# A two-layer transformer on one core: weights split in whole buffers of 2048 columns instead of halves

## The chip, the cores and the metric

The kernel runs on one core of one Trainium2 chip. The metric is device time in microseconds. The engines are TensorE (PE in the profile; its weight loads are PEld), VectorE (DVE), ScalarE (ACT), GpSimd (POOL) and SyncE (SP, which issues most of the loads).

## The reference

Input is one sequence of 256 tokens of width 1024 in float32. Two layers run one after the other, each of three blocks that add to the residual `x`:

```python
for l in range(2):
    x = x + 0.5 * swiglu(rms_norm(x, ffa_norm[l]), ffa_w_gate[l], ffa_w_up[l], ffa_w_down[l])
    x = x + hybrid_mixer(rms_norm(x, mix_norm[l]), w_in[l], ..., w_out[l])
    x = x + 0.5 * swiglu(rms_norm(x, ffb_norm[l]), ffb_w_gate[l], ffb_w_up[l], ffb_w_down[l])
return rms_norm(x, final_norm)
```

`swiglu` is `(silu(x @ w_gate) * (x @ w_up)) @ w_down` with an inner width of 2816. `hybrid_mixer` projects to 2840 columns (`w_in`), runs two kinds of attention on 8 heads each, and projects back with `w_out`. All weights are float32, and each is used once, so each comes once from memory.

## The kernel before

**Split products.** Every float32 product is made of three matmuls of a rounded type (`F32R`). A factor w is split into `whi`, its rounded copy, and `wlo`, the rest `w - whi`; `prod3` (lines 321 to 326) adds x-high times w-high (line 323), x-high times w-low (line 324) and x-low times w-high (line 325) into one PSUM bank. `prod_t` (lines 334 to 343, matmuls at 340 to 342) is the same with the weight as the stationary side. So weights have to be split on the way: ACT copies raw columns into `whi` (line 304), DVE subtracts (line 283). `xhi`/`xlo`, `hhi`/`hlo`, `nhi`/`nlo`, `ohi`/`olo` and `fnhi`, `fohi` are split left sides.

**Units.** Weights come in units of at most 2048 columns on 128 partitions, 1 MB each. A unit is loaded by one transfer, mostly, into one of five `raw` buffers (`loader`), or is added by a transfer onto the raw buffer that holds an earlier unit (`adder`, line 263, issued by POOL). `Unit` holds the state of one: `part(i)` gives the slices of high and low for row block i, `when(i)` the event after which they may be read. Before, a unit's high and low lie in two pairs of tiles of 1024 columns (`halves`). There are NW = 6 such tiles for `whi` and six for `wlo`; one token of the pool `"w"` stands for a pair, and `free_w` gives one back. Most units are split 1024 columns at a time (`step` = 2 quarters). The units of Q, D and E in the mixer (`grouped`) and the first two of the program (`fine`) are split a quarter at a time, 512 columns.

**Who orders the work.** The program's order on every engine is written out by a planner (`Flow`) that runs when the kernel is built: coroutines yield events or buffer tokens, each engine has a modelled clock, and among those that are due the one with the lowest rank goes first. It decides only the order in which instructions are put into each engine's queue; on the chip each engine takes its own queue in order and waits for the semaphores of its operands. `splitter` (lines 268 to 306, rank 4) walks the units in order: it waits until ACT and DVE are nearly free, writes the DVE subtraction of the piece before (`low`), waits for the landed raw columns and a token, and writes the ACT copy of the next piece. The main coroutine walks the products in a fixed order and waits for `when(i)`.

**The stages.** In an FFN, gate and up columns run in the order of `PLANS`: names such as `g2` or `u2` are two units each whose quarters meet both token halves, 24 matmuls of 512 columns for a unit; names such as `51` are one unit with one token block, 12 matmuls. The down projection follows `DOWN`: `1d` to `7d` are units of 12 matmuls, `p2` to `p10` units of 24. At the end of an FFN (`TAIL`) the units `p7` and `p10` are walked once for each of four output banks and stay held to the end, and `4d` is used ahead of the fourth of these walks. In the mixer, the projections `A Q B D E F`, the attention, and the output projection `out_prod` follow; that holds both units of a half (first n, then m) until all of its four banks are done. After each block, `close` or `out_close` adds to `x`, `Norm.pair` turns `x` (line 409), makes `xhi` and `xlo` (lines 415, 418) and squares (line 431) for the next block.

Of the kernel before, what the change touches and what calls it, by code (L numbers as in the profile page):

```python
# [9 lines left out]
F32R = mybir.dt.float32r  # L10
I32 = mybir.dt.int32
BF16 = mybir.dt.bfloat16
AF = mybir.ActivationFunctionType
# [121 lines left out]
def hybrid_kernel(ctx, tc, x_in, ffa_norm, ffa_w_gate, ffa_w_up, ffa_w_down, mix_norm, w_in,  # L135
# [3 lines left out]
    nc = tc.nc  # L139
# [3 lines left out]
    wts = ctx.enter_context(tc.tile_pool(name="wts", bufs=4))  # L143
# [4 lines left out]
    ctx.enter_context(tc.manual_schedule())  # L148

    fl = Flow()  # L150
    NRAW, NW, NP = 5, 6, 5
    for tag, n in (("acc", 4), ("sb", 2), ("tb", 2), ("raw", NRAW), ("w", NW),
                   ("work", 7), ("p", NP), ("pT", 4), ("pair", 1)):
        fl.pool(tag, range(n))
# [22 lines left out]
    class Raw:  # L177


        def __init__(self, src, a, b, loads=1):  # L180
            self.src, self.a, self.b, self.loads = src, a, b, loads
            self.landed = [Event() for _ in range(4)]
            raws.append(self)
# [15 lines left out]
    class Unit:  # L199
# [3 lines left out]
        def __init__(self, raw, done=True, fine=False, grouped=False):  # L203
            self.raw, self.a, self.b = raw, raw.a, raw.b
            self.done, self.grouped = done, grouped
            self.step = 1 if fine or grouped else 2
            self.ready, self.halves = [Event() for _ in range(4)], []
            self.over = Event()
            units_.append(self)

        def part(self, i):

            k = self.a // 2
            return [z[:, i % k * self.b:(i % k + 1) * self.b] for z in self.halves[i // k]]

        def when(self, i):
            return self.ready[4 * (i + 1) // self.a - 1]
# [50 lines left out]
    def splitter():  # L268

        def view(u, z, i, turned=False):  # L270
            m = u.a * u.b // 4
            z = z[:, i % 2 * m:(i % 2 + u.step) * m]
            if not u.grouped:
                return z
            return z.rearrange("p (r g d) -> p g r d" if turned else "p (g r d) -> p g r d", r=4, g=2)

        def source(u, i):
            src = u.raw.rows(i, u.step)
            return src.rearrange("p (g r d) -> p g r d", g=2, r=4) if u.grouped else src

        def low(u, i, t):
            hi, lo = u.halves[i // 2]
            nc.vector.tensor_tensor(view(u, lo, i, True), source(u, i), view(u, hi.bitcast(F32), i, True), OP.subtract)  # L283
            e = fl.dve(u.step * u.a * u.b // 4, after=t)
            for j in range(i, i + u.step):
                u.ready[j].set(e)
            if i + u.step == 4:
                u.over.set(e)
                if u.done:
                    fl.put("raw", 0, e)  # L290

        last = None
        for u in units_:
            for i in range(0, 4, u.step):
                yield max(fl.eng["act"], fl.eng["dve"]) - (TH if fl.clock > 16.0 else TH0)
                if last is not None:
                    low(*last)
                    last = None
                yield u.raw.landed[i + u.step - 1]
                if i % 2 == 0:  # L300
                    yield fl.get("w")
                    u.halves.append(tuple(wts.tile([128, 1024], F32R, name=z, tag=z, bufs=NW) for z in ("whi", "wlo")))
                n = u.step * u.a * u.b // 4
                nc.scalar.activation(view(u, u.halves[-1][0], i, True), source(u, i), AF.Copy)  # L304
                last = (u, i, fl.act(n))
        low(*last)

    def copy(dst, src, n):
# [3 lines left out]
        nc.vector.tensor_copy(dst, src)  # L312
        return fl.dve(n)

    def free_w(u=None):
        fl.put("w", 0)

    def cols(w, c0, n, kh):
        return w[kh * 512:(kh + 1) * 512, c0:c0 + n].rearrange("(k p) n -> p k n", p=128)
# [171 lines left out]
    def ffn(us, nm, nxt, plan, last=False):  # L491
# [103 lines left out]
        def plain(z, tag, first):  # L595
            c, then = int(z[1:]), {"g": gate, "u": up, "h": both}[z[0]]
            ps = {}
            for kh in range(2):
                u = us[z, kh]
                order_ = [(t, i) for t in range(T) for i in range(4)] if first and nm.gi else [(t, i) for i in range(4) for t in range(T)]  # L600
                for t, i in order_:
                    k = kh * 4 + i
                    yield nm.turned[k, t]
                    yield u.when(i)
                    if k == 0:
                        yield fl.get(tag)
                        ps[t] = bank(tag, 4 if tag == "acc" else 2)
                    prod(ps[t], nm.xs, t, k, u, i, slice(0, 512), k == 0, k == KT - 1)
                    if k == KT - 1:
                        fl.spawn(then(c, t, ps[t], tag))  # L610
                    yield
                    if t and i % 2:
                        free_w()
# [55 lines left out]
        def product(p, c):  # L669
            u = us[p, c]  # L670
            key = dict(zip("1265374", "aabccdd"))[p]
            if p == "1":
                fl.spawn(rest(c))
                fl.spawn(gate0(c))
            start = p in "1657"
            k0, t = {"1": (0, 0), "2": (4, 0), "4": (4, 1)}.get(p, (0, 0))
            if p in "124":
                left = [z[:, k0:k0 + 4, t * 128:(t + 1) * 128] for z in nm.xs]
                for k in range(k0, k0 + 4):
                    yield nm.turned[k, t]  # L680
            else:
                yield event("form", p)
                left = forms[p]
            if not start:
                yield event(key, c)
            for i in range(4):
                yield u.when(i)
                if i == 0 and start:
                    yield fl.get("acc")
                    bk[key, c] = bank("acc", 4)  # L690
                wh, wl = u.part(i)
                prod3(bk[key, c], left[0][:, i], left[1][:, i], wh, wl, start and i == 0, i == 3)
                yield
                if i % 2:
                    free_w()
            event("P" + p, c).set(fl.clock + HOP)
# [67 lines left out]
        def down(j, t, cs, free):  # L764
            u = us["d", j]
            yield ev[j // 2, t]
            for c in cs:
                new = yield from bank_d(t, c)
                for i in range(2):
                    k = 2 * j + i  # L770
                    yield u.when(i)
                    prod(pd[t, c], hs, t, k, u, i, slice(c * 512, (c + 1) * 512), new and i == 0, k == 21)
                    yield
            if free:
                free_w()
                free_w()
# [961 lines left out]
    for q in range(4):  # L1738
        fl.spawn(start_x(q))
    fl.spawn(loader(), 3)  # L1740
    fl.spawn(splitter(), 4)
    fl.spawn(adder(), 3)
    fl.spawn(main(), 5)
# [38 lines left out]
```

## Time and profile before

| what | us |
|---|---|
| median of 2 runs | 993.69 (993.49 to 993.89) |
| the profiled execution | 991.77 |
| its span, first to last instruction | 990.0 |
| busy: PE, DVE, ACT, POOL | 980.0, 799.9, 643.4, 68.9 |
| weights and inputs read | 215.09 MB |

Busy time counts an engine from the start of an instruction to its end. Matmuls overlap in the pipeline and their ends are modelled, so for PE the distance from start to start is to be read, not only the busy share. In a timeline row the note in brackets is the idle time of the engine ahead of that row and what ended it.

### The profile page before, as it was taken

How to read it: one execution, taken by the hardware profiler on the slowest of the kernel's cores; microseconds unless marked ns; L12 is line 12 of the kernel's file. 1: busy time of each engine (PE TensorE's matmuls, PEld its weight loads, DVE VectorE, ACT ScalarE, POOL GpSimd, SP SyncE). 2: the span in 40 equal slices, each digit the busy share in tenths (PEclk: the TensorE clock that was granted, in tenths of full speed). 3: DMA queues.
4: the chain of work that ended last, by engine and by line, in shares of the span. 5: the costliest groups of instructions: out<-in, count | busy, mean ns of one | idle time of the engine just before them, and what ended most of it. 6: DMA issues, size and time to landing. Idle time of an engine off the chain costs nothing.

```text
span 990.0 us, 14315 instructions
## 1 busy us (share of the span) xinstructions
PE 980.0 (99%) x5236; PEld 820.0 (83%) x5236; DVE 799.9 (81%) x1458; ACT 643.4 (65%) x1101; POOL 68.9 (7%) x73
## 2 busy tenths in 40 slices
PE   9999999999999999999999999999999999999997
PEld 8888888898987888888888888888988878888885
DVE  6977786797887978798798778877878789688976
ACT  7665555568785676666567566646787766665654
POOL 1010001100000011101001110101000001110110
PEclk9999999999999999999999999999999999999999
DMA  9889679463743699989859999893645337999891
GB/s 336 267 211 282 221 196 288 127 217 115 265 138 116 188 252 287 259 255 244 258 174 238 293 272 253 228 302 110 225 170 200 101 128 216 278 272 278 252 213 43
DMA packets 109831, 217.08 MB, mean 219 GB/s; under 512 B 3928, under 2 KB 23520, under 8 KB 109760
## 3 DMA queue, kind: packets, MB, share of 16 engines
q1 hardware_dynamic: 85584, 168.50, 48.6%
q0 software_dynamic: 23872, 47.12, 27.0%
q8 instruction: 41, 0.67, 0.3%
q10 hardware_dynamic: 304, 0.53, 0.1%
q14 instruction: 30, 0.25, 0.1%
HBM read 215.09 MB, written 1.05 MB: 218 GB/s over the span
## 4 chain that ended last, share of the span: by engine, by line
PE 98%; DVE 1%; ACT 1%; issue 0%; POOL 0%; POOLq 0%
PE acc L323 18%; PE acc L324 18%; PE acc L325 18%; PE sb L325 8%; PE sb L323 8%; PE sb L324 8%; PE acc L340 2%; PE acc L341 2%; PE acc L342 2%; PE tb L555 2%; PE acc L1209 2%; PE tb L1189 2%; PE tb L409 1%; PE acc L1378 1%; PE sb L1315 1%; PE sb L1258 1%
## 5 line engine op out<-in xcount | busy, mean ns | idle before, releaser
L283 DVE TENSOR_TENSOR wlo<-raw,whi 128x1024 fp32r<-128x1024 f32 (+2 forms) x422 | 472.2, 1139 | 116.3 <-ACT whi L304 115.7
L304 ACT ACTIVATE whi<-raw 128x1024 fp32r<-128x1024 f32 (+2 forms) x422 | 408.6, 993 | 200.6 <-PE acc L325 75.3
L323 PE MATMUL acc<-whi,xhi 128*128 128x512 f32 (+1 forms) x372 | 145.8, 392 | 0.0
L324 PE MATMUL acc<-wlo,xhi 128*128 128x512 f32 (+1 forms) x372 | 142.0, 382 | 0.0
L325 PE MATMUL acc<-whi,xlo 128*128 128x512 f32 (+1 forms) x372 | 141.9, 381 | 0.0
L323 PE MATMUL sb<-whi,xhi 128*128 128x512 f32 x288 | 113.1, 393 | 0.0
L325 PE MATMUL sb<-whi,xlo 128*128 128x512 f32 x288 | 112.2, 390 | 0.0
L324 PE MATMUL sb<-wlo,xhi 128*128 128x512 f32 x288 | 112.1, 389 | 0.0
L323 PE MATMUL acc<-whi,hhi 128*128 128x512 f32 x256 | 100.9, 394 | 0.0
L325 PE MATMUL acc<-whi,hlo 128*128 128x512 f32 x256 | 99.8, 390 | 0.0
L324 PE MATMUL acc<-wlo,hhi 128*128 128x512 f32 x256 | 99.7, 389 | 0.0
L325 PEld LDWEIGHTS acc<-whi,xlo 128*128 128x128 f32 x372 | 69.9, 188 | 13.5
L323 PEld LDWEIGHTS acc<-whi,xhi 128*128 128x128 f32 x372 | 70.1, 189 | 12.6 <-issue 0.7
L324 PEld LDWEIGHTS acc<-wlo,xhi 128*128 128x128 f32 x372 | 70.0, 188 | 11.9
L325 PEld LDWEIGHTS sb<-whi,xlo 128*128 128x128 f32 x288 | 54.1, 188 | 11.4
L324 PEld LDWEIGHTS sb<-wlo,xhi 128*128 128x128 f32 x288 | 54.1, 188 | 11.0
L323 PEld LDWEIGHTS sb<-whi,xhi 128*128 128x128 f32 x288 | 54.1, 188 | 10.9
L340 PE MATMUL acc<-xhi,whi 128*128 128x256 f32 x192 | 56.6, 295 | 0.0
L325 PEld LDWEIGHTS acc<-whi,hlo 128*128 128x128 f32 x256 | 48.1, 188 | 10.2
L324 PEld LDWEIGHTS acc<-wlo,hhi 128*128 128x128 f32 x256 | 48.1, 188 | 9.7
L323 PEld LDWEIGHTS acc<-whi,hhi 128*128 128x128 f32 x256 | 48.1, 188 | 9.5
L342 PE MATMUL acc<-xhi,wlo 128*128 128x256 f32 x192 | 54.2, 282 | 0.0
(267 smaller groups left out, 1618.5 us busy)
## 6 DMA issues: line engine op xcount, KB each, us to landing
raw<-in_ffa_w_down_dram SPq DMA_DIRECT2D x20, 1024.0 KB, 5.4
raw<-in_w_in_dram SPq DMA_DIRECT2D x20, 1024.0 KB, 5.7
raw<-in_ffb_w_gate_dram SPq DMA_DIRECT2D x20, 1024.0 KB, 5.7
raw<-in_ffb_w_down_dram SPq DMA_DIRECT2D x20, 1024.0 KB, 7.8
raw<-in_ffa_w_gate_dram SPq DMA_DIRECT2D x18, 1024.0 KB, 7.3
raw<-in_ffa_w_up_dram SPq DMA_DIRECT2D x17, 1024.0 KB, 7.4
raw<-in_ffb_w_up_dram SPq DMA_DIRECT2D x16, 1024.0 KB, 6.2
raw<-in_ffb_w_up_dram POOLq DMA_DIRECT2D x12, 1024.0 KB, 9.3
```

Source lines behind the costliest of these rows:

```text
L283: nc.vector.tensor_tensor(view(u, lo, i, True), source(u, i), view(u, hi.bitcast(F32), i, True), OP.subtract)
L304: nc.scalar.activation(view(u, u.halves[-1][0], i, True), source(u, i), AF.Copy)
L323: nc.tensor.matmul(ps, xh, wh, start=first, stop=False, skip_group_check=True)
L324: nc.tensor.matmul(ps, xh, wl, start=False, stop=False, skip_group_check=True)
L325: nc.tensor.matmul(ps, xl, wh, start=False, stop=last, skip_group_check=True)
L340: nc.tensor.matmul(ps, wh, xs[0][:, k], start=first and j == 0, stop=False, skip_group_check=True)
L341: nc.tensor.matmul(ps, wh, xs[1][:, k], start=False, stop=False, skip_group_check=True)
L342: nc.tensor.matmul(ps, wl, xs[0][:, k], start=False, stop=last, skip_group_check=True)
L409: nc.tensor.transpose(ps[:, i * n + (t - ts[0]) * 128:i * n + (t - ts[0] + 1) * 128], x[:, t, k * 128:(k + 1) * 128], ident)
L555: nc.tensor.transpose(ps[:, j * 128:(j + 1) * 128], h[:, j * 128:(j + 1) * 128], ident)
L1189: nc.tensor.transpose(ps[:, j * 128:(j + 1) * 128], pp[:, i * n + s_ * 128:i * n + (s_ + 1) * 128], ident)
L1209: nc.tensor.matmul(grp.o[u * 64:(u + 1) * 64, h // 2 * 128:(h // 2 + 1) * 128], val(s_), pT[:, j * 128:(j + 1) * 128], start=u not in grp. ...
```

## The change

A unit's high and low now lie in one pair of tiles of 2048 columns, of which there are three for each part; the bytes are the same. One ACT copy and one DVE subtraction now split the whole unit (`step` = 4), except for Q, D, E and the first two units, whose quarters are still split one by one, into one tile. `free_w` gives a token back at every second call, so a buffer comes free when both halves of its unit have been used.

```diff
-    NRAW, NW, NP = 5, 6, 5
+    NRAW, NW, NP = 5, 3, 5
...
-            self.step = 1 if fine or grouped else 2
-            self.ready, self.halves = [Event() for _ in range(4)], []
+            self.step = 1 if fine or grouped else 4
+            self.ready, self.parts = [Event() for _ in range(4)], None
...
         def part(self, i):
 
-            k = self.a // 2
-            return [z[:, i % k * self.b:(i % k + 1) * self.b] for z in self.halves[i // k]]
+            return [z[:, i * self.b:(i + 1) * self.b] for z in self.parts]
...
             m = u.a * u.b // 4
-            z = z[:, i % 2 * m:(i % 2 + u.step) * m]
+            z = z[:, i * m:(i + u.step) * m]
...
-            hi, lo = u.halves[i // 2]
+            hi, lo = u.parts
...
-                if i % 2 == 0:
+                if i == 0:
                     yield fl.get("w")
-                    u.halves.append(tuple(wts.tile([128, 1024], F32R, name=z, tag=z, bufs=NW) for z in ("whi", "wlo")))
+                    u.parts = tuple(wts.tile([128, 2048], F32R, name=z, tag=z, bufs=NW) for z in ("whi", "wlo"))
                 n = u.step * u.a * u.b // 4
-                nc.scalar.activation(view(u, u.halves[-1][0], i, True), source(u, i), AF.Copy)
+                nc.scalar.activation(view(u, u.parts[0], i, True), source(u, i), AF.Copy)
...
-    def free_w(u=None):
-        fl.put("w", 0)
+    used = [0]
+
+    def free_w():
+
+        used[0] += 1
+        if used[0] % 2 == 0:
+            fl.put("w", 0)
```

## Rows read from the trace of the kernel before

**Rows 1.** The page, part 1: busy microseconds of each engine, share of the span.

```profile
PE 980.0 (99%) x5236; PEld 820.0 (83%) x5236; DVE 799.9 (81%) x1458; ACT 643.4 (65%) x1101; POOL 68.9 (7%) x73
```

**Rows 2.** The page, part 4: the chain that ended last, by engine.

```profile
PE 98%; DVE 1%; ACT 1%; issue 0%; POOL 0%; POOLq 0%
```

**Rows 3.** Waits of PE: who waited for whom, total, times, longest.

```profile
PE acc L324 <- DVE wlo L283: 1.6, 2, 0.8
```

**Rows 4.** Groups by line and shape: busy us, mean ns, idle before.

```profile
L283 DVE TENSOR_TENSOR wlo<-raw,whi 128x1024 fp32r<-128x1024 f32 x358 | 429.4, 1219 | 112.7 <-ACT whi L304 112.4
L304 ACT ACTIVATE whi<-raw 128x1024 fp32r<-128x1024 f32 x358 | 370.3, 1057 | 186.4 <-PE acc L325 75.3 <-PE sb L325 49.0 <-DMA raw<-in_ffb_w_up_dram 17.5
...
L283 DVE TENSOR_TENSOR wlo<-raw,whi 128x512 fp32r<-128x512 f32 x56 | 37.6, 685 | 3.6 <-ACT whi L304 3.4
...
L304 ACT ACTIVATE whi<-raw 128x512 fp32r<-128x512 f32 x56 | 33.8, 626 | 10.7 <-PE acc L341 7.9 <-DMA raw<-in_ffa_w_gate_dram 2.6
```

**Rows 5.** Timeline of PE, FFN to FFN: start us, us, instruction.

```profile
495.11 0.39 PE L325 MATMUL acc<-whi,hlo 128*128 128x512 f32 x1
495.34 0.39 PE L323 MATMUL acc<-whi,hhi 128*128 128x512 f32 x1
...
498.29 0.39 PE L324 MATMUL acc<-wlo,xhi 128*128 128x512 f32 x1
```

**Rows 6.** Timeline of ACT over the same exit.

```profile
493.52 1.06 ACT L304 ACTIVATE whi<-raw 128x1024 fp32r<-128x1024 f32 x1 [0.57 <-ACT junk L431]
494.85 1.14 ACT L415 ACTIVATE xhi<-tb,gall 128x128 fp32r<-128x128 f32 x4 [0.27 <-PE tb L409]
495.86 0.65 ACT L431 ACTIVATE junk<-x 128x512 f32<-128x512 f32 x1
...
496.48 2.97 ACT L304 ACTIVATE whi<-raw 128x1024 fp32r<-128x1024 f32 x3
```

**Rows 7.** Timeline of DVE over the same exit.

```profile
494.61 1.23 DVE L283 TENSOR_TENSOR wlo<-raw,whi 128x1024 fp32r<-128x1024 f32 x1 [0.51 <-ACT whi L304]
...
498.72 0.68 DVE L847 SCALAR_TENSOR_TENSOR x<-acc,x 128x512 f32<-128x512 f32 x1
```

**Rows 8.** Timeline of ACT, exit of the first FFN into the mixer.

```profile
188.48 2.96 ACT L304 ACTIVATE whi<-raw 128x1024 fp32r<-128x1024 f32 x3
```

**Rows 9.** Timeline of PE, output projection from half n to half m.

```profile
301.85 0.39 PE L325 MATMUL acc<-whi,nlo 128*128 128x512 f32 x1
...
306.74 0.40 PE L324 MATMUL acc<-wlo,ohi 128*128 128x512 f32 x1
...
308.39 0.50 PE L324 MATMUL acc<-wlo,ohi 128*128 128x512 f32 x1 [0.80 <-DVE wlo L283]
```

**Rows 10.** Timeline of ACT at that change of halves.

```profile
302.18 1.05 ACT L304 ACTIVATE whi<-raw 128x1024 fp32r<-128x1024 f32 x1
```

**Rows 11.** Timeline of DVE at that change of halves.

```profile
304.34 1.21 DVE L283 TENSOR_TENSOR wlo<-raw,whi 128x1024 fp32r<-128x1024 f32 x1
```

**Rows 12.** Timeline of PE around unit p10, second FFN.

```profile
479.84 0.39 PE L325 MATMUL acc<-whi,hlo 128*128 128x512 f32 x1
...
484.38 0.39 PE L324 MATMUL acc<-wlo,hhi 128*128 128x512 f32 x1
```

**Rows 13.** Timeline of DVE around p10.

```profile
480.68 2.36 DVE L283 TENSOR_TENSOR wlo<-raw,whi 128x1024 fp32r<-128x1024 f32 x2 [1.17 <-ACT whi L304]
```

**Rows 14.** Timeline of DVE before the product 5d.

```profile
453.04 0.68 DVE L729 TENSOR_TENSOR fnlo<-a,fnhi 128x512 fp32r<-128x512 f32 x1
```

**Rows 15.** Timeline of PE at the first matmul of 5d.

```profile
455.59 0.39 PE L323 MATMUL sb<-whi,fnhi 128*128 128x512 f32 x1
```

**Rows 16.** One stretch: us, busy and count of each engine, clock, DMA, GB/s.

```profile
810.00:840.00 30.00, 30.00 (x138) 24.87 (x137) 28.89 (x48) 20.48 (x26) 2.60 (x2) 1.00 0.72 210
```

**Rows 17.** Stretches after the last matmul: busy of each engine, clock, DMA, GB/s.

```profile
983.40:985.70 2.30, 0.00 (x0) 0.00 (x0) 1.95 (x6) 1.02 (x3) 0.00 (x0) 1.00 0.00 0
985.80:990.00 4.20, 0.00 (x0) 0.00 (x0) 0.52 (x2) 0.72 (x1) 0.00 (x0) 0.50 0.33 125
```

## The prediction, made before the changed kernel was run

> **What bounds the kernel now.** I read the page first. PE is busy for 980.0 of the 990.0 us [rows 1], and the chain that ended last runs 98% over PE, with 1% each on DVE and ACT [rows 2]. A busy share alone can deceive here, so next come the waits of PE: for the split weights it waited twice, 1.6 us in all [rows 3]. The timeline then shows it working at full pitch: at an FFN's end its matmuls start 0.23 us apart, and from the first product after `4d` to the first L324 of the next block lie 13 matmuls in 498.29 - 495.34 = 2.95 us [rows 5], 0.227 us for each. So the kernel is as long as its row of matmuls, which the change leaves as it is. ACT and DVE count only where they make PE wait, and there is next to nothing left to win. That both stand idle in places is the normal state: ACT was idle for 186.4 us ahead of its 1024-column copies, most of it until PE had given a buffer back [rows 4]. The buffers are full and the splits wait for PE, not PE for the splits. The question is thus how much of that cover the coarser buffers use up.
>
> **What one whole split costs.** A DVE subtraction takes 685 ns for 512 columns and 1219 ns for 1024 [rows 4], so 534 ns for each further 512, and 1219 + 2 x 534 = 2287 ns for 2048. An ACT copy takes 626 and 1057 ns [rows 4], and 1057 + 2 x 431 = 1.92 us for 2048. The count falls from 358 pieces of 1024 to 179 of 2048. On DVE this removes 179 x (2 x 1.219 - 2.287) = 27 us, on ACT 179 x (2 x 1.057 - 1.92) = 35 us. I put both at zero, since PE hides them all: it lost 1.6 us to this work in the whole run.
>
> The Trainium skill, page "VectorE: DVE Perf Modes", section "The TRN2 errata", has operations that read SBUF pay a fixed extra cost for each instruction, which speaks for fewer and larger ones. The rows agree that there is such a cost, 0.15 us a piece here; what would follow for the time is the last rival below.
>
> **What the round through a buffer costs.** A buffer is read by PE, freed, copied into by ACT, subtracted by DVE, and read again. For a unit of 12 matmuls before: 6 x 0.227 = 1.36 us of reading, 1.06 ACT, 1.22 DVE and 0.1 for the three hand-overs (ACT's copy ended at 493.52 + 1.06 = 494.58 [rows 6] and DVE began at 494.61 [rows 7]), 3.7 us; six halves last PE 6 x 1.36 = 8.16 us, so 4.4 us are spare. After: 2.72 + 1.92 + 2.29 + 0.1 = 7.0 us against 3 x 2.72 = 8.16: 1.1 us spare. With a unit of 24 matmuls in the round (5.44 us), three buffers last PE at least 10.9 us and more than 3.8 us are spare. Inside a stage I therefore expect the cover to hold, thinly, at nothing. If it is gone, that is the second rival below.
>
> **Leaving an FFN.** Here the cover is gone for certain. `p7` and `p10` are held to the last, so the next block's first unit must take the buffer of `4d`. Before, its first half began at 493.52, as soon as the first half of `4d` was read, and its second half came after the turning of `x` [rows 6]. After, the whole copy waits for the last matmul of `4d`, which ends at 495.11 + 0.39 = 495.50 [rows 5]. ACT is then turning `x` (four copies from 494.85) and squaring (from 495.86); before, the next split began at 496.48 [rows 6]. With the copy in that place: 496.48 + 1.92 = 498.40, DVE to 500.69. PE wants the low part at 498.29 [rows 5], so it waits 2.4 us. Were the copy written ahead of the squaring, it would be 0.6 us less (495.86 + 1.92 + 2.29 = 500.07); were DVE's closing addition (0.68 us, at 498.72 [rows 7]) written ahead of the subtraction, 0.7 us more. What is queued behind the waiting copy on ACT is the squaring and the last turn of `x`; behind the longer DVE piece, that addition, on which the turn hangs, which the first 24 matmuls of the late unit cover. So 1.8 to 3.1 us an exit, I take 2.4. This happens three times: into the first mixer (where ACT shows the same row, 188.48 [rows 8]), FFN to FFN, and into the second mixer. Sum: 3 x 2.4 = **+7.2** (5.4 to 9.3).
>
> **p10.** It takes the buffer of `p6`, last read at 479.84 + 0.39 = 480.23 [rows 12]. Copy and subtraction: 480.25 + 1.92 + 2.29 = 484.46, wanted at 484.38 [rows 12]. Before, DVE made both halves in a row from 480.68 [rows 13]. That is 0.1 us in each of four FFNs, **+0.4**; with one DVE operation of 0.7 us ahead of it, 0.8 each, 3.2.
>
> **From half n to half m.** Both units of n are held; the second unit of m waits. Before, its first half was copied from 302.18 [rows 10], just as the last matmul on the first unit of n ended (301.85 + 0.39 = 302.24 [rows 9]); its second half came late, and PE stood 0.80 us at 308.39 [rows 9]; so in both mixers, 1.6 us [rows 3]. After: copy 302.25 to 304.17, subtraction from 304.34, where DVE took the first half before [rows 11], to 306.63, wanted at 306.74 [rows 9]. Both halves are then there, and the wait is gone: **-1.6**. With one 0.7 us operation ahead, 0.6 us of waiting stay in each mixer and the gain is 0.4 us for both; with two, 1.3 us each, a loss of 1.0 us for both.
>
> **Product 5d.** Its left side is ready at 453.04 + 0.68 = 453.72 [rows 14] and read at 455.59 [rows 15], 1.87 us later. It is made by a row of DVE operations between subtractions. A whole subtraction that slips in where a half did costs 1.07 us: covered. Two of them: 0.3 us, three times in the run. I take 0, bound +0.9. The loads, SP's queue and POOL's adds move by the same one or two us; a raw buffer is returned when its whole unit is split, as before, so I put them at zero as long as PE's cover holds.
>
> **The sum** is 7.2 + 0.4 - 1.6 = +6.0 us: the profiled execution would go from 991.77 (its span of 990.0 and 1.77 around it) to 997.8. It lies 1.92 us under the median of the runs, so the median goes from 993.69 to **999.7**. By the bounds: 5.4 + 0 - 1.6 = +3.8 to 9.3 + 3.2 + 1.0 + 0.9 = +14.4, or 997.5 to 1008.1.
>
> **Rivals.** *The planner fits it in.* The order is made anew, and PE has transposes to do at each exit. If they fill the wait, or the copy gets ahead of the turns, and the wait at m goes, it ends between 992.1 (993.69 - 1.6, the most that can be won) and 995. Against it: the exit's wait starts from the last matmul of `4d`, which no order moves. Chance 0.12.
>
> *DVE falls behind inside the stages.* This ends on the slow side. DVE is busy for 28.89 of 30 us in one stretch [rows 16], and every late eviction now stands behind up to 2.29 us. It decides where a round of three 12-matmul units has more than 1.1 us of other DVE or ACT work in it, two operations of 0.68 [rows 7]. The plans hold 13 such rounds, four in each of the last three FFNs (`51 21 31`, `61 71 13` and two in `41 53 23 33`) and one in the first. If each loses one and a half operations beyond that, 1.1 us, it is 999.7 + 14.3 = 1014.0. For it: the stretch above. Against it: the same stretch shows PE unbroken, total DVE time falls, and a 24-matmul unit comes after every three or four. Chance 0.20, half of it over 1013.6 us.
>
> *The clock falls.* After the last matmul the granted clock is still 1.00 up to 985.70 and 0.50 from 985.80, some 2.4 us after PE stopped [rows 17]; that is 2.4 to 1.2 GHz. A wait of 2.4 us at each exit is as long. If the clock falls there, the matmuls of the next 12 to 24 (2.7 to 5.4 us at full speed, my guess of the time to recover, as no row shows one) take twice as long: 3 x 4 = +12, or 1011.7. Chance 0.06. The Trainium skill, "TensorE: Matmul & The Clock Gate", Part 1, says the same in kind: an idle array is gated down, and work opens it again.
>
> *The change doesn't do what it says* would show as more than 179 whole copies; the diff leaves little room for it, 0.02, at 993.7.
>
> *The saved instructions shorten the run*, by the 27 us of DVE: 967. PE's wait of 1.6 us [rows 3] is all that speaks for it, its 980.0 us of work against it: 0.01.
>
> **How the numbers follow.** The forecast of 999.7 has 0.59, with its bounds. The range is 993 to 1010: it leaves out the upper part of the second and third rivals (0.17) and the last us below. Faster by over 2% (under 973.8) is the last rival: 0.01. Slower by over 2% (over 1013.6): 0.10 of the second rival and 0.02 of the third. 2% is about what a measurement of this kernel can tell from no change.
>
> **What would show it.** In the profile after, the waits of PE on L283 should list three of about 2.4 us at the FFN exits, none at m, four tiny ones at `p10`, and the copies should stand at 1.92, the subtractions at 2.29 us. Many waits between 0.3 and 1.5 us inside the FFNs would prove the second rival; a granted clock under 1 at an exit the third. I am wrong if the exit's wait is filled, or if the planner's new order delays evictions in ways that the old one doesn't show.

## The result, and the profile after

The changed kernel takes 1024.97 us, median of 2 runs (1024.01 to 1025.94), against 993.69 before: ratio 1.0328, interval 1.0310 to 1.0347. It is slower by 31 us, where 999.7 was forecast and the range ended at 1010. The profiled execution took 1025.94 us with a span of 1024.1, which is 34.1 us more than the span of before; the profiled execution of before had been 1.92 us under the median of its runs, and this one is 1 us over.

The page of the changed kernel, part 1 (busy time) and part 4 (the chain that ended last, by engine):

```profile
PE 995.1 (97%) x5236; PEld 825.0 (81%) x5236; DVE 791.9 (77%) x1289; ACT 616.6 (60%) x904; POOL 68.9 (7%) x73
...
PE 95%; ACT 2%; DVE 2%; issue 0%; POOL 0%; POOLq 0%
```

Against [rows 1, 2]: PE has the same 5236 matmuls, DVE 169 instructions fewer and ACT 197 fewer, and both are busy for less time. PE is still nearly the whole chain, but it is now busy for 15 us more with the same matmuls, a first sign that some of them ran slower. The groups by line and shape (busy us, mean ns, idle time before and its releaser) have the whole pieces:

```profile
L282 DVE TENSOR_TENSOR wlo<-raw,whi 128x2048 fp32r<-128x2048 f32 x179 | 409.7, 2289 | 155.6 <-ACT whi L303 155.1
L303 ACT ACTIVATE whi<-raw 128x2048 fp32r<-128x2048 f32 x179 | 342.8, 1919 | 239.4 <-PE acc L329 99.3 <-PE sb L329 55.3 <-issue 50.5
```

The three matmuls of `prod3` are now lines 327 to 329, the copy is line 303, the subtraction line 282. The waits of PE (total us, times, longest), where before had one row that matters [rows 3]. A wait of 1.4 us at the program's start, the same in every kernel here, is left out of these lists:

```profile
PE sb L327 <- ACT fnhi L731: 7.6, 3, 2.5
PE acc L328 <- DVE wlo L282: 5.5, 3, 1.8
PE sb L329 <- DVE fnlo L733: 5.0, 3, 1.7
PE tb L413 <- DVE v L354: 1.5, 2, 0.8
PE acc L327 <- ACT p L635: 1.1, 3, 0.4
```

The second row holds the three forecast waits on leaving an FFN. The first and the third are new: the left side of the product `5d` is late in the last three FFNs, first its high part (`fnhi`), then its low part (`fnlo`). The timeline of PE at `5d` in the second FFN (start us, duration, instruction, idle time before and its releaser):

```profile
460.27 0.39 PE L329 MATMUL acc<-whi,hlo 128*128 128x512 f32 x1
463.18 0.50 PE L327 MATMUL sb<-whi,fnhi 128*128 128x512 f32 x1 [2.52 <-ACT fnhi L731]
463.52 0.40 PE L328 MATMUL sb<-wlo,fnhi 128*128 128x512 f32 x1
465.59 0.80 PE L329 MATMUL sb<-whi,fnlo 128*128 128x512 f32 x1 [1.68 <-DVE fnlo L733]
466.18 0.63 PE L327 MATMUL sb<-whi,fnhi 128*128 128x512 f32 x1
466.61 0.63 PE L328 MATMUL sb<-wlo,fnhi 128*128 128x512 f32 x1
```

Two things are to be seen: the two waits, and that the matmuls from 466.18 start 0.43 us apart instead of 0.227. Stretches of the same place, and one at the exit from the second FFN to the third (busy time and count of PE, PEld, DVE, ACT, POOL, then the granted clock, DMA share, GB/s):

```profile
460.00:463.80 3.80, 1.28 (x5) 0.50 (x4) 2.19 (x3) 3.10 (x4) 0.00 (x0) 1.00 1.10 208
464.00:470.60 6.60, 5.01 (x12) 3.95 (x13) 3.34 (x5) 0.98 (x3) 1.28 (x1) 0.50 1.01 248
470.80:480.00 9.20, 9.20 (x42) 7.59 (x41) 4.28 (x2) 5.09 (x4) 0.00 (x0) 1.00 0.60 165
507.00:517.00 10.00, 8.16 (x36) 6.06 (x36) 8.19 (x14) 8.75 (x15) 0.00 (x0) 1.00 0.31 99
```

The granted clock is 0.50 from 463.8 for 6.8 us, at its level of 1.2 GHz. It falls so five times: at `5d` in three FFNs, and on leaving the first and the third FFN into a mixer. The exit at 512 us, with as long a wait, keeps 1.00.

**Where 34.1 us went.** I compared the start of each product's second matmul in both traces; how far it has moved at one place less how far at the place before is what the stretch between them cost.

| place | us |
|---|---|
| product `5d` in the last three FFNs (7.0, 6.3, 7.0) | +20.3 |
| leaving an FFN, three times 2.2 | +6.6 |
| inside each of the last three FFNs, about 1.0 | +2.9 |
| both mixers, from the first product to `u0` of the next FFN | +2.7 |
| `p10`, four times 0.19 | +0.8 |
| the rest | +0.7 |

The clock is inside these rows: by my estimate from the starts, the slowed matmuls cost 1.46, 2.10, 1.20, 1.49 and 2.11 us over the 0.227 us of full speed, 8.4 us in all, of which 5.4 lie at `5d` and 2.95 in the mixers.

**Why `fnhi` and `fnlo` are late.** Eight additions on DVE (L720 four times, then L739, 741, 743, 745) make the sums for four products. The program writes `fnhi` and `fnlo` behind the last of them, and the planner puts subtractions of weights between these steps. The timeline of DVE before `5d` in the changed kernel:

```profile
439.43 0.68 DVE L720 TENSOR_TENSOR a<-hhi,hlo 128x512 f32<-128x512 f32 x1
...
453.28 0.69 DVE L739 TENSOR_TENSOR a<-a 128x512 f32<-128x512 f32 x1
454.04 2.29 DVE L282 TENSOR_TENSOR wlo<-raw,whi 128x2048 fp32r<-128x2048 f32 x1
456.25 0.69 DVE L741 TENSOR_TENSOR a<-a 128x512 f32<-128x512 f32 x1
456.85 0.69 DVE L566 TENSOR_TENSOR hlo<-tb,hhi 128x512 fp32r<-128x512 f32 x1
457.45 2.28 DVE L282 TENSOR_TENSOR wlo<-raw,whi 128x2048 fp32r<-128x2048 f32 x1
459.65 0.68 DVE L743 TENSOR_TENSOR a<-a 128x512 f32<-128x512 f32 x1
460.37 0.69 DVE L745 TENSOR_TENSOR a<-a 128x512 f32<-128x512 f32 x1
462.64 2.29 DVE L282 TENSOR_TENSOR wlo<-raw,whi 128x2048 fp32r<-128x2048 f32 x1 [1.57 <-ACT whi L303]
464.85 1.29 DVE L733 TENSOR_TENSOR fnlo<-a,fnhi 128x512 fp32r<-128x512 f32 x2
```

From the first addition to `fnlo` it takes 25.4 us, and six whole subtractions in it take 13.2 (starts of the next instruction counted). Before, the same stretch was 17.8 us long, with eight halves of 9.1 us in it, and ended at the 453.04 of [rows 14].

This longer row is not itself what PE waited for. In the code the sum that `5d` needs is complete with L739 (L735 before), the first of the last four; the three behind it serve other products. The trace of the kernel before agrees: there `fnhi` began ahead of the last of the eight.

```profile
444.36 0.68 DVE L735 TENSOR_TENSOR a<-a 128x512 f32<-128x512 f32 x1
450.01 0.62 ACT L727 ACTIVATE fnhi<-a 128x512 fp32r<-128x512 f32 x1
450.17 0.68 DVE L741 TENSOR_TENSOR a<-a 128x512 f32<-128x512 f32 x1
```

In the changed kernel this sum was there at 453.28 + 0.69 = 453.97. But `fnhi`, written late, stands in ACT's queue behind two copies:

```profile
455.24 1.92 ACT L303 ACTIVATE whi<-raw 128x2048 fp32r<-128x2048 f32 x1 [0.75 <-PE acc L329]
460.70 1.91 ACT L303 ACTIVATE whi<-raw 128x2048 fp32r<-128x2048 f32 x1 [3.54 <-PE acc L329]
462.51 1.13 ACT L731 ACTIVATE fnhi<-a 128x512 fp32r<-128x512 f32 x2
```

The second copy waited 3.54 us for a buffer that PE gave back with its last matmul ahead of `5d` (460.27 + 0.39 = 460.66). From there both waits can be followed: the copy runs for 1.91 us, then `fnhi`, and PE starts at 463.18; the subtraction of the same unit runs from 462.64 for 2.29 us, then `fnlo`, and PE goes on at 465.59. So the split of one whole unit stands ahead of the left side in both queues, and it could begin only when PE had nothing left to do before `5d`. The unit is one for a later product, as PE read the low part for `5d` at 463.52, while this subtraction was still running. Before, `fnhi` began 5.6 us ahead of the 455.59 of [rows 15].

### The profile page after: what moved, and what is told of

The parts are those of the page before. It is cut to its first block, busy times and chain, and to the rows that moved or that the text cites. A ratio compares the mean times of both kernels' runs of the same rounds, so it can differ in the third digit from the quotient of the medians.

```text
span 1024.1 us, 13772 instructions
## 1 busy us (share of the span) xinstructions
PE 995.1 (97%) x5236; PEld 825.0 (81%) x5236; DVE 791.9 (77%) x1289; ACT 616.6 (60%) x904; POOL 68.9 (7%) x73
## 4 chain that ended last, share of the span: by engine, by line
PE 95%; ACT 2%; DVE 2%; issue 0%; POOL 0%; POOLq 0%
PE acc L327 18%; PE acc L328 18%; PE acc L329 18%; PE sb L329 8%; PE sb L327 8%; PE sb L328 8%; PE acc L344 2%; PE acc L345 2%; PE acc L346 2%; PE tb L559 2%; PE acc L1213 2%; PE tb L1193 2%; DVE wlo L282 1%; ACT whi L303 1%; PE tb L413 1%; PE acc L1382 1%
## 5 line engine op out<-in xcount | busy, mean ns | idle before, releaser
L282 DVE TENSOR_TENSOR wlo<-raw,whi 128x2048 fp32r<-128x2048 f32 (+2 forms) x239 | 452.4, 1897 | 158.1 <-ACT whi L303 157.6
L303 ACT ACTIVATE whi<-raw 128x2048 fp32r<-128x2048 f32 (+2 forms) x239 | 380.9, 1604 | 266.5 <-PE acc L329 100.0
L345 PE MATMUL acc<-xlo,whi 128*128 128x256 f32 x192 | 54.2, 282 | 0.0
```

Of the source, the lines that this page charges most:

```text
L303: nc.scalar.activation(view(u, u.parts[0], i, True), source(u, i), AF.Copy)
L345: nc.tensor.matmul(ps, wh, xs[1][:, k], start=False, stop=False, skip_group_check=True)
```

## The experiments

Theory: the planner counts a subtraction as one step, so that a chain of steps with subtractions between them grows with the piece; `5d` has the tightest chain, its cover of 1.87 us is passed, and the waits take the clock down. "The chain" below is the stretch on DVE from the first addition to `fnlo`; by the rows above it counts through the place that it gives `fnhi` and `fnlo` in the queues. Rivals: the coarser release of buffers makes everything late (the bytes held, not the length of the pieces); or DVE simply lacks time in the last FFN stages. Diffs are against the changed kernel, except for the last. The experiments ran on chips on which the kernel before takes 992.0 to 992.5 us, so a difference against the 1024.97 can be off by 1 to 2 us.

**1. Half pieces in whole buffers.** The buffers are released whole as in the changed kernel, but are filled in two pieces of 1024.

```diff
-            self.step = 1 if fine or grouped else 4
+            self.step = 1 if fine or grouped else 2
```

> Three whole buffers as in the change, but each unit is again split in two pieces of 1024 columns. Theory (the size of the piece on ACT and DVE makes the left side of 5d and the first unit after an FFN late): the waits at 5d fall under 1 us each, those at the three exits to about 0.4 us, the clock stays up, 996 to 1000 us. Rival (a buffer that comes back only as a whole is the cause; ACT's copy stands waiting for it with the left side's copies behind it): 5d still waits 3 us or more three times and the clock falls there, 1010 to 1020 us.

998.35 us against 992.34 on the same chip, ratio 1.0053 (1.0039 to 1.0066). The waits of PE in this kernel:

```profile
PE acc L328 <- DVE wlo L282: 4.4, 8, 1.2
```

No wait at `5d`, the chain 19.3 us with eight halves of 9.1 us, no drop of the clock. So release by whole buffers costs 5 to 6 us by itself, and the length of the pieces the other 25 or so. The first rival is out as the main cause. Each exit costs 0.55 us here, but the waits from half n to half m remain (1.2 us in each mixer, 0.8 before).

**2. `5d` later.** Only the place of `5d` in the order of the down projection moves, behind `p9`, which gives its left side 5.4 us (24 matmuls) more.

```diff
-DOWN = "1d p2 2d p8 5d p9 3d p3 6d p6 7d p7 p10 4d".split()
+DOWN = "1d p2 2d p8 p9 5d 3d p3 6d p6 7d p7 p10 4d".split()
```

> The change, with 5d behind p9, one unit of 24 matmuls (5.4 us) later. Theory (the left side of 5d is some 4.9 us late, and three waits there with the clock that falls in them carry two thirds of the loss): the waits at 5d vanish and with them 17 us of half clock, 1000 to 1004 us. Rival (the splits as a whole are behind there): the wait moves to p9 or 3d and more than 1015 us are left.

1004.91 us, ratio 1.0112 (1.0082 to 1.0142): 20 us less than the changed kernel and 0.9 us over what was expected. The waits of PE:

```profile
PE acc L328 <- DVE wlo L282: 5.5, 3, 1.8
PE tb L413 <- DVE x L1564: 1.5, 2, 0.8
PE acc L327 <- ACT p L635: 1.1, 3, 0.4
```

The chain is as long as in the changed kernel (25.4 us), and the waits for `fnhi` and `fnlo` are gone: the copy ahead of `fnhi` now runs while PE works on `p9`. The clock falls only at the two mixer exits. What was lost at `5d` was a deadline, not DVE's time. The second rival is out.

**3. Filled waits.** 21 extra matmuls ahead of each `5d` and 9 ahead of the first product after an FFN, into a bank that the real product then overwrites. This adds PE work that the reference doesn't need and changes no result.

```diff
+    def fill(ps, left, u, n):
+
+        for _ in range(n):
+            nc.tensor.matmul(ps, left, u.part(0)[0][:, :512], start=True, stop=True, skip_group_check=True)
...
+                    if p == "5":
+                        fill(ps, hs[0][:, 0, :128], u, 21)
...
+                        if name == "A" and k == 0 and t == 0:
+                            fill(ps[t], xs[0][:, 0, :128], u, 9)
```

> The change, with matmuls put into the waits whose results are overwritten: 21 (4.8 us) ahead of 5d in the last three FFNs and in the first, 9 (2.0 us) ahead of the first product of the first units after an FFN. Every other engine keeps its order. Theory (a wait costs its length and then the half clock behind it): the clock stays at 1.00 and 12 us of half clock are saved, less 4.8 us in the first FFN, where there was no wait: 1016 to 1019 us. Rival (the clock that falls costs nothing beside the waits): 1025 to 1030 us.

1021.76 us, ratio 1.0280 (1.0249 to 1.0310). The stretch at `5d`:

```profile
458.00:475.00 17.00, 17.00 (x77) 13.97 (x76) 12.53 (x12) 8.17 (x8) 2.56 (x2) 1.00 0.89 196
```

The clock stays at 1.00 through `5d` and the exits, so the falls do come from PE's idle time. The gain is smaller than expected: 1016 to 1019 us was the theory, 1025 to 1030 the rival, and the time lies between them. The fill costs 4.75 us in the first FFN, where nothing waited; at the other places each fall of the clock that is gone gives back 1.5 to 2.2 us, 9.1 in all (1.6, 1.6 at the exits into the mixers, 2.2, 1.5, 2.2 at `5d`), near the 8.4 from the slowed starts and under the 12 that the expectation took.

**4. The chain unbroken.** All eight additions are put into DVE's queue in a row; four lines like this one:

```diff
-            yield fl.dve(512)
+            fl.dve(512)
```

> The change, with DVE's eight additions for the left sides of 5d, 6d, 3d and 7d put into its queue in two unbroken rows, so that no subtraction of 2048 columns can come between those of a row. Theory (those subtractions make the left side late): 5d waits under 1 us, 1000 to 1005 us. Rival (ACT's copy that waits for its buffer ahead of the left side's copies makes it late): 5d still waits 2 us or more, over 1015 us.

1012.73 us, ratio 1.0204 (1.0162 to 1.0247), where 1000 to 1005 was expected. The chain is now 9.2 us long with one subtraction in it, and `5d` waits for nothing. Another wait took its place. Waits of PE:

```profile
PE tb L559 <- DVE sg L594: 6.0, 3, 2.0
```

Two instructions on `sg`, which belong ahead of `1d`, now stand behind the unbroken row of additions. PE waits 2.0 us for them in three FFNs, and the clock falls twice (444.9 and 943.3); at the three exits, with 1.82 us of waiting each, it stays at 1.00. The theory's place is right, but the cure only moved the deadline that is missed.

**5. Copies whole, subtractions in halves.** The subtraction is put into DVE's queue as two pieces of 1024, at two steps of the splitter.

```diff
+            n = min(u.step, 2)
+            m = u.a * u.b // 4
...
-            e = fl.dve(u.step * u.a * u.b // 4, after=t)
...
+            e = fl.dve(n * m, after=t)
...
+                    if last[0].step == 4:
+                        yield max(fl.eng["act"], fl.eng["dve"]) - TH
+                        low(last[0], 2, last[2])
```

> The change, but DVE subtracts each unit in two pieces of 1024 columns, put into its queue at two steps, so that other DVE work can go between; ACT still copies 2048 at once. Theory (each of the additions for the left side of 5d stands behind a subtraction of 2.29 us): the wait at 5d falls from 4.9 to 1.5 us or less, the wait at an exit from 2.1 to about 1.1, the clock stays up, 1000 to 1006 us. Rival (ACT's copy of 1.92 us ahead of the left side's copies): 5d still waits 3 us, over 1015 us.

1010.87 us against 992.52, ratio 1.0190 (1.0174 to 1.0205), where 1000 to 1006 was expected. The chain is 19.3 us with eight halves, `5d` is not among the waits, and the clock doesn't fall. But the exits cost 2.25 us as in the changed kernel, where 1.1 was expected, since a subtraction can't start before the whole copy ends. There are also new waits, which cost 3.0 us each, at the first `u0` of two FFNs:

```profile
PE acc L339 <- DVE wlo L286: 14.4, 15, 2.0
```

**6. Copies in halves, subtractions whole.** The counterpart of 5.

```diff
-                nc.scalar.activation(view(u, u.parts[0], i, True), source(u, i), AF.Copy)
-                last = (u, i, fl.act(n))
+                if u.step == 4:
+                    for h in range(2):
+                        if h:
+                            yield max(fl.eng["act"], fl.eng["dve"]) - TH
+                        sl = slice(h * n // 2, (h + 1) * n // 2)
+                        nc.scalar.activation(u.parts[0][:, sl], u.raw.rows(2 * h, 2), AF.Copy)
+                        last = (u, i, fl.act(n // 2))
...
```

> The change, but ACT copies each unit in two pieces of 1024 columns at two steps; DVE still subtracts 2048 at once. Theory (DVE's piece is what counts): 5d still waits 4 us, the exits 2 us, 1018 to 1028 us. Rival (ACT's piece): under 1010 us.

1029.89 us, ratio 1.0371 (1.0350 to 1.0392), the slowest of all. A miss for my theory as I had put it: whole subtractions should have kept the wait at `5d`, and it is gone. Waits of PE:

```profile
PE acc L336 <- DVE wlo L282: 15.0, 8, 2.8
PE sb L336 <- DVE wlo L282: 5.4, 3, 1.8
```

In this order only four whole subtractions (8.8 us) fell into the chain, which is 18.6 us long, and `fnhi` begins 4.2 us ahead of `5d`. So it is not the length of a subtraction alone that makes `5d` late, but what the planner's order puts ahead of its left side. What the kernel loses instead is the weights: PE waits for low parts eleven times, 2.8 us at the worst, and the clock falls three times. The step that now stands between the two copies of a unit puts off its subtraction; that this alone explains the waits I did not test.

**7. Both cures.** `5d` behind `p9` as in 2, and the units of the first product of each of the five blocks that follow another (`exit`) split in halves; all others whole.

```diff
-DOWN = "1d p2 2d p8 5d p9 3d p3 6d p6 7d p7 p10 4d".split()
+DOWN = "1d p2 2d p8 p9 5d 3d p3 6d p6 7d p7 p10 4d".split()
...
-            self.step = 1 if fine or grouped else 4
+            self.step = 1 if fine or grouped else 2 if exit else 4
```

> The change, with 5d behind p9 as in the run with 5d later, and the first unit after an FFN split in two pieces. Theory (the exits cost 2.2 us of waiting each, and two of them 1.7 us of half clock): 1004.9 less 3 times 1.6 less 2 times 1.7, 996 to 998 us, clock at 1.00 throughout. Rival (the wait at the exit comes from the buffer that is given back late and not from the size of the piece): 1003 to 1005 us.

997.05 us, ratio 1.0048 (1.0031 to 1.0065), as expected. Waits of PE:

```profile
PE acc L328 <- DVE wlo L282: 1.4, 5, 0.6
PE acc L327 <- ACT p L635: 1.1, 3, 0.4
```

The exits cost 0.3 to 0.4 us, the clock never falls. The place of one product and the first units of five blocks thus hold 27 of the 31 us; of what is left, 4.5 us, some 3 are the 1.0 inside each of three FFNs.

**8. Only the second row unbroken.** As 4, but for L739 to L745 alone, so that what belongs ahead of `1d` keeps its place.

> The change, with only the second row of four additions for the left sides of 5d, 6d, 3d and 7d put into DVE's queue unbroken; the first row stays open to other work. Theory (two whole subtractions, 4.6 us, stand between these four and are two thirds of what made 5d's left side late): the waits at 5d fall from 4.9 to about 0.5 us, no new wait ahead of 1d, 1003 to 1008 us. Rival (the subtractions that leave this row come back ahead of it or behind it, before the low part of 5d's left side): 5d still waits 2.5 us or more, 1013 us or more.

1007.34 us against 992.00, ratio 1.0142 (1.0118 to 1.0166), within what was expected. The timeline of DVE:

```profile
452.78 0.68 DVE L739 TENSOR_TENSOR a<-a 128x512 f32<-128x512 f32 x1
453.49 0.69 DVE L741 TENSOR_TENSOR a<-a 128x512 f32<-128x512 f32 x1
454.22 0.69 DVE L743 TENSOR_TENSOR a<-a 128x512 f32<-128x512 f32 x1
454.95 0.69 DVE L745 TENSOR_TENSOR a<-a 128x512 f32<-128x512 f32 x1
```

And on ACT:

```profile
453.88 0.62 ACT L731 ACTIVATE fnhi<-a 128x512 fp32r<-128x512 f32 x1
```

Two whole subtractions left the chain (four of 8.8 us remain, 19.4 us in all), and neither `5d` nor `1d` waits. This saves 17.6 us against the changed kernel, with no piece made shorter. The sum for `5d` is there at 452.78 + 0.68 = 453.46, hardly earlier than the 453.97 of the changed kernel; but `fnhi` begins at 453.88 and not at 462.51, since the program comes to write it ahead of the two copies. So the place in the queues is what the wait hung on. In the other runs it fits: in the second FFN `fnhi` begins 0.7 us ahead of `5d`'s first matmul in the changed kernel, and 3.4 us or more ahead in the runs in which `5d` doesn't wait and isn't filled (6.0 in run 1, 3.4 in 2 and 7, 19 in 4, 6.4 in 5, 4.2 in 6, 6.1 here). No run moved `fnhi` and `fnlo` alone. What stays is the exits, 2.2 us each, at which the clock now falls all three times (192.9, 507.0, 691.3), and one new wait of 1.2 us at 490.13.

**9. The kernel before, with earlier release.** One thing that the prediction had found in the kernel before is mended there: `out_prod` held both units of half n until all banks were done; here each is given back after its last product. This diff is against the kernel before.

```diff
+                        if t and c and k % 2:
+                            free_w()
+                            free_w()
                     fl.spawn(out_close(key, t, c, ps, last))
-            for _ in range(4):
-                free_w()
```

> The kernel before, with the first unit of an output projection's half given back when its last product is written and not with the second unit. Theory (the 0.8 us wait of PE in each mixer comes from a split that is put into the queues too late): that wait goes, 1.6 us less than before, ratio 0.998 to 0.999. Rival (the wait only moves): within 0.5 us of before.

990.16 us against 992.00, ratio 0.9976 (0.9966 to 0.9986), faster than both kernels. Waits of PE:

```profile
PE tb L555 <- DVE sg L580: 0.9, 1, 0.9
PE sb L1528 <- DVE sq L1523: 0.8, 2, 0.4
```

The two waits of [rows 3] are gone; one of 0.9 us and two of 0.4 came elsewhere, so the sum of the waits is no smaller. In the profiled executions the gain is 0.8 us.

Four whole buffers for each part, which would give the release more room, were not tried.

## Why the prediction was wrong

**The step that failed is the one on the product `5d`**: "I take 0, bound +0.9". It measured 20.3 us, of which 12.6 are waits that the profile lists, 5.4 the half clock, and the rest the restarts. The prediction named the row of DVE operations, its cover of 1.87 us and the price of one exchanged subtraction (1.07), counted at most two exchanges, and left the order and ACT out. What the trace showed in its place is the split of one whole unit ahead of the left side: a copy of 1.91 us ahead of `fnhi`, a subtraction of 2.29 us ahead of `fnlo`, and both begin only once PE has finished all its work before `5d`, so that nothing covers them. How it came there is the planner's order. The stretch to `fnlo` on DVE grew by 25.4 - 17.8 = 7.6 us, 4.1 of it for six whole subtractions in place of eight halves, 3.0 for idle time, most of it ahead of subtractions that waited for ACT's copies, and 0.4 for the rest; the left side, which the program writes behind this row, slipped behind one more unit. Runs 2, 8 and 4 show it from three sides: the deadline moved, the left side written earlier, the row nearly without subtractions. A small misreading was in the step too: at 455.59 PE reads the high part, and `fnlo` first at 456.04, so that the cover of `fnlo` was 2.3 us.

**Leaving an FFN** was right: 2.2 us each for 2.4, in the place foretold. The timeline at the second exit:

```profile
510.45 0.51 PE L327 MATMUL acc<-whi,xhi 128*128 128x512 f32 x1
512.77 0.50 PE L328 MATMUL acc<-wlo,xhi 128*128 128x512 f32 x1 [1.82 <-DVE wlo L282]
```

Run 7 shows that halves at these first units bring it down to 0.3 to 0.4.

**The clock** was put as a rival at the exits with 0.06 and 12 us. It fell at two of the three exits and three times at `5d`, and cost 8.4 us. The mechanism was right in kind and its chance too low: [rows 17] already showed the clock falling after an idle time like the one that the sum forecast three times. The size of 4 us a fall was two to three times too large, 1.2 to 2.1 measured. The Trainium skill, "TensorE: Matmul & The Clock Gate", Part 1, was cited for an idle array being gated down and opened again by work; the rows above agree, 1.00 to 0.50 and back, apart from the exit at 512 us, which kept 1.00.

**From half n to half m**: the wait of 0.8 us in each mixer did go, but the gain did not stay. As the block ends, PE now waits for DVE ahead of turning `x` (L413, the fourth row of its waits, 0.8 us each). A forecast of -1.6 for both; without the half clock of 2.95, the +2.7 of the mixers is -0.2.

**Inside the FFNs** the first forecast of 0 came out as +2.9. What can be named is the last row of PE's waits, 0.4 us in each of three FFNs. ACT's timeline there:

```profile
405.38 1.92 ACT L303 ACTIVATE whi<-raw 128x2048 fp32r<-128x2048 f32 x1 [0.80 <-PE acc L329]
...
407.81 0.57 ACT L635 ACTIVATE p<-acc 128x512 f32<-128x512 f32 x1
```

An eviction that frees a bank (L635) stands behind a whole copy. In run 5, with copies as long, PE doesn't wait here, so the length of the copy alone is not shown to be the cause. This is the second rival in kind, at a fifth of its 14.3 us and not in the rounds of three 12-matmul units where it was put: there PE waited for no weights. The remaining 0.6 us of each are restarts and small shifts that I did not take apart.

**Right without more**: the pieces (2287 ns and 1.92 us forecast, 2289 and 1919 measured), that less work on ACT and DVE brings nothing, and `p10` (0.1 each forecast, 0.19 measured). The work that went was less than the 27 and 35 us worked out from durations: busy time fell by 8.0 us on DVE and 26.8 on ACT.

## What to carry to other kernels

When a piece in a queue gets longer, throughput and the round through its buffer are only half of the check. For every step that another engine waits for, look at what the program's order puts just ahead of it, on each engine that it crosses, and ask what that piece itself waits for. If it waits for a buffer that the consumer gives back last, its whole length is added to the wait, however early the step's own inputs are there. Read from the code which inputs those are: the instruction just before is not always one of them. And a wait of some 2 us on TensorE may cost as much again through the clock (1.2 to 2.1 us a fall here).

## What was not expected of the hardware

A wait of about 2 us is enough to lose the clock, but not always. On leaving an FFN, PE waited 1.82 us each time; the granted clock fell to 0.50 twice for 3.4 us and stayed at 1.00 once in the changed kernel. In run 8, with the same wait, it fell all three times (there PE had also waited 1.19 us at 490.13, 16 us ahead of the second exit). In run 4, again with 1.82 us, it stayed at 1.00 at all three exits, and so it did in run 5, with 1.94 to 1.97 us. At `5d`, with two waits, it was 0.50 for 6.8, 3.4 and 6.8 us. At that level matmuls of 512 columns start 0.43 us apart instead of 0.227. In four of the changed kernel's five falls the clock drops after PE is back at work, as at 463.8, when it had started again at 463.18 (the fifth came at 655.0, at the end of the second wait); so most of the price is paid by matmuls that wait for nothing. What tells the exits that kept their clock from those that didn't is open.
